# A hybrid attention and delta-rule layer on one core: new operation times in the list that lays out the order of instructions

## The chip, the cores and the metric

One core of a Trainium2 chip. The metric is the device time of one execution in microseconds (us); the median of three runs is given. The engines are TensorE (PE; its weight loads appear as PEld), VectorE (DVE), ScalarE (ACT), GpSimd (POOL) and SyncE (SP), which issues the DMAs. Each runs its own queue of instructions in program order and waits on semaphores for the others.

## The reference

One layer of a streaming encoder over 2048 prompt frames and 32 new frames, D = 1024, in float32. A LayerNorm of the input is projected to 6160 columns. Two branches read them:

```python
qa, ka, va, za, qkv_b, zb, a_b, b_b, gate_a, gate_b = split_projection(x @ w_in)
oa = chunk_band_attention(qa, ka, va, rel_bias)          # 8 heads of 64, band of 9 chunks of 64 frames
ya = (oa * silu(za)) @ w_branch_a
c  = silu(causal_conv(qkv_b, conv_w))                    # width 4; q and k are then L2-normalised
ob = gated_delta_rule(qb, kb, vb, g, beta, state)        # chunks of 64 frames, 8 heads
yb = (rms_norm(ob) * silu(zb)) @ w_branch_b
mix = sigmoid(gate_a) * ya + sigmoid(gate_b) * yb
y = layer_norm(ALPHA * x + mix @ w_out)
```

The delta rule takes a triangular solve for each chunk (all chunks independent), and then a recurrence over chunks:

```python
t_inv = triangular_solve(eye + m, eye)
v_new = u_c - w_c @ s
o_c   = (q_c * exp(gc_c)) @ s + qk_c @ v_new
s     = s * exp(g_last) + k_dec.T @ v_new
```

## The kernel before

**Staging.** The sequence is cut in two halves of 1024 frames (the second also has the 32 new frames). For each half the kernel runs the delta-rule branch (`phase_b`), then attention (`phase_a`). The input projection is cut into 48 column blocks of 128 and one of 16; each block of each half is a "job" whose weights are fetched, split into a high and a low fp16 part (`whi`, `wlo`), and multiplied as three fp16 products (hi·hi, hi·lo, lo·hi) into a PSUM bank `pj` of up to 512 columns. Jobs are the filler of PE: their order is written by hand (`ORDER`, `FILL`, `HEAD`, `TAIL`: 16 delta-rule jobs in the order q, k, v, z, with gate jobs between and behind them, then 16 attention jobs, then the remaining gate jobs). In the second half the branch products run in fp32r beside attention, and the output projection and last LayerNorm close the kernel.

**Delta-rule phase.** For each of 4 head pairs and 2 blocks of 8 chunks: the convolution (three DVE steps on tile `acc`), the decays, products of keys and queries out of PSUM (`p_c`, `qk_bd`, `kd_bd`, `v_t`), a forward substitution on DVE (`substitute`: for 31 columns one product into `sys_t` and one subtraction from `sys_u`, up to some 76 elements a lane; two systems can be in work at once), and the recurrence (`chain`). A step of the recurrence for a chunk is a loop of three hops between PE and DVE: matmul of the state into tile `x`, DVE step `r`; matmul into `x`, DVE step `vn`; matmul into `x`, DVE step `state`. Two more matmuls a chunk go into tile `o`, which ACT copies to `v_t`. There are 128 chunks of the prompt (two heads in each) and 4 of the new frames, so 132. An fp32 matmul appears as two records in the trace.

**What sets the order.** No instruction order is written out. Every activity is a Python generator, a stream, with a clock. `Flow` is a planner: it keeps a heap of streams and always resumes the one with the earliest clock. When a stream issues an instruction, `Flow.spend` (line 194) sets the instruction's planned end: the later of the stream's clock plus a hop and the engine's planned free time, plus a cost from `Engine.price` (line 232). That end becomes the clock of the stream and the free time of the engine. The hops are constants: 0.1 us to PE, 0.2 us to another engine, 0.12 us to the same engine. DMAs have planned landing times too (`Flow.transfer`), and gates hand out buffers and PSUM banks in planned time. The order in which streams are resumed is the program order of every engine's queue and of the DMA queue; nothing else of the plan is in the program. On the chip each instruction waits for its real inputs, behind everything that stands before it in its queue.

**What the change touches.** `Engine.price` alone. It returns microseconds from the operation's name, sizes and memory: on PE from the columns that stream (n) and the result rows (m) by type; on ACT and DVE from a fixed part, larger or smaller when an operand lies in PSUM (`far`), and the elements per lane n at 1200 or 960 (1920) per us; on GpSimd (key `"G"`) likewise. All instructions pass through line 267, in the helper `call`, so that the profile shows L267 for nearly every line; instructions are told apart by tile.

Of the kernel before, what the change touches and what calls it, by code (L numbers as in the profile page):

```python
# [13 lines left out]
F16 = mybir.dt.float16  # L14
# [7 lines left out]
P = 128  # L22
D = 1024
KD = D // P
# [6 lines left out]
HD = 64  # L31
# [187 lines left out]
def width(ap):  # L219
    n = 1  # L220
    for k in ap.shape[1:]:
        n *= k
    return n


class Engine:
# [5 lines left out]
    def price(self, name, a, k):  # L232

        if self.key == "PE":
            n, m = width(a[2]), width(a[1])
            if name == "transpose":
                n = m = max(a[1].shape[0], m)
            if a[1].dtype == F16:
                return max(n / 2400.0, m / 4800.0)
            if a[1].dtype == F32R:  # L240
                return n / 2400.0
            return max(n, m) / (1200.0 if name == "transpose" else 600.0)
        ins = [k[x] for x in ("in_", "in0", "in1") if x in k] or list(a[1:2])
        out = k["out"] if "out" in k else a[0]
        n = width(ins[0] if name in ("bn_stats", "tensor_reduce") else out)
        far = any(getattr(x, "space", None) == PSUM for x in ins + [out])
        if self.key == "G":
            if k.get("op") == ALU.pow:
                return 0.55 + 0.125 * n
            return 0.03 + n / 1200.0 if name == "memset" else 0.1 + n / (960.0 if name == "affine_select" else 480.0)  # L250
        more = sum(not isinstance(k.get(x, 0.0), (int, float, type(None)))
                   for x in ("scale", "bias", "accum_out", "scalar1", "scalar2"))
        if self.key == "S":

            table = k.get("func") == AF.Ln
            if "func" in k and table != self.table and k["func"] != AF.Copy:
                self.table = table
                return 1.28 + self.price(name, a, k)
            return (0.05 if far else 0.093) + 0.093 * more + n / 1200.0
        fast = name in ("tensor_copy", "tensor_scalar") and not far  # L260
        return (0.125 if far else 0.068) + 0.06 * more * fast + n / (1920.0 if fast else 960.0)

    def __getattr__(self, name):
        f = getattr(self.eng, name)
# [2277 lines left out]
```

## Time and profile before

| | |
|---|---|
| Median of 3 runs | 1968.77 us (1964.63 to 1972.47) |
| The profiled execution's own time | 1967.06 us |
| Its span, first to last instruction | 1965.2 us |
| Instructions in it | 40968 |
| DMA | 274.61 MB, 140 GB/s on average |

A profile line of a group names line, engine, operation, result<-inputs and shapes, then the count, busy time in us and mean length of one in ns, and behind the second bar the time its engine sat idle just before, with who released it. Lines of the timeline begin with start and length in us. A matmul's record is longer than its step to the next matmul, since matmuls are pipelined; so the busy time of PE also covers part of the time it waits. In lines on waits stand the total in us, how many times, and in some views the longest.

### The profile page before, as it was taken

To read this page: it belongs to the slowest core of one execution; us is meant where nothing else is said; L and a number is where in the kernel's file an instruction comes from. 1 tells how busy PE (TensorE), PEld (TensorE's weight loads), DVE (VectorE), ACT (ScalarE), POOL (GpSimd) and SP (SyncE) were. 2 spreads that over 40 slices of the span, in tenths; PEclk is the share of its full clock that TensorE was granted. 3 is DMA by queue.
4 is the path that set the end of the run, shared out by engine and by line. 5 is a ranking of instruction groups with operands and counts; after the bars stand their busy time and mean duration, and the time that the engine had idled before them with its cause. 6 is when DMAs were issued, how large, how long until landed. Compare 5 with 4: busy or idle time off the path is not lost. (4 is left out here: it accounts for less than half of the span.)

```text
span 1965.2 us, 40968 instructions
## 1 busy us (share of the span) xinstructions
PE 1894.8 (96%) x14513; PEld 1339.0 (68%) x14513; DVE 1409.0 (72%) x4401; ACT 993.6 (51%) x2022; POOL 771.2 (39%) x1079
## 2 busy tenths in 40 slices
PE   8999999999999998999999999999999999999998
PEld 5445666676455556666776777768877667988886
DVE  7689989973378768679898987355556565465797
ACT  6665545544586777565544444354446575321110
POOL 7344334433344445444344333422222233243673
PEclk9999999999999999999999999999999999999999
DMA  3234232333368887223233233477878798996552
GB/s 134 69 89 114 78 108 68 84 90 105 115 154 203 179 185 168 75 81 84 58 79 93 67 91 103 120 206 189 223 190 172 184 198 187 263 331 200 179 183 89
DMA packets 382950, 274.61 MB, mean 140 GB/s; under 512 B 248339, under 2 KB 319359, under 8 KB 382745
## 3 DMA queue, kind: packets, MB, share of 16 engines
q1 hardware_dynamic: 382744, 272.00, 51.9%
q8 instruction: 114, 1.87, 0.4%
q14 instruction: 92, 0.75, 0.1%
HBM read 157.15 MB, written 71.76 MB: 116 GB/s over the span
## 5 line engine op out<-in xcount | busy, mean ns | idle before, releaser
L267 PE MATMUL pj<-hi,whi 128*128 128x512 f16 (+2 forms) x1992 | 643.0, 338 | 11.6 <-DVE zb L267 3.1
L267 PE MATMUL pj<-hi,wlo 128*128 128x512 f16 (+2 forms) x1952 | 634.5, 338 | 0.6 <-POOL wlo L267 0.5
L267 PEld LDWEIGHTS <-whi 128*128 128x128 f16 x3984 | 408.8, 104 | 229.0 <-issue 9.6
L267 POOL TENSOR_TENSOR wlo<-wraw,whi 128x256 f16<-128x256 f32 (+1 forms) x392 | 281.4, 740 | 466.9 <-ACT whi L267 380.7
L267 PE MATMUL pj<-lo,whi 128*128 128x512 f16 (+2 forms) x1992 | 453.0, 338 | 0.0
L267 PEld LDWEIGHTS <-wlo 128*128 128x128 f16 x1952 | 204.9, 105 | 116.2 <-issue 13.2
L267 ACT ACTIVATE sb<-sb,mx,unit 128x640 f32<-128x640 f32 (+4 forms) x128 | 108.6, 849 | 101.1 <-DVE mx L267 96.0
L267 POOL TENSOR_TENSOR pu<-sb,pu 128x640 f16<-128x640 f32 (+2 forms) x64 | 82.2, 1284 | 177.6 <-ACT pu L267 135.5
L267 ACT ACTIVATE wraw<-wraw,w_scale 128x1024 f32<-128x1024 f32 (+1 forms) x98 | 111.4, 1137 | 78.1 <-DVE w_scale L267 75.8
L267 ACT CAST whi<-wraw 128x512 f16<-128x512 f32 (+2 forms) x212 | 128.2, 611 | 28.0 <-PE pj L267 24.9
L267 DVE TENSOR_TENSOR sys_u<-sys_u,sys_t 128x60 f32<-128x60 f32 (+24 forms) x527 | 124.8, 242 | 5.7
L267 DVE SCALAR_TENSOR_TENSOR acc<-raw,cwT,acc 128x512 f32<-128x512 f32 x144 | 112.4, 781 | 7.9 <-ACT acc L267 6.5
L267 DVE TENSOR_TENSOR sys_t<-sys_u,sys_p 128x60 f32<-128x60 f32 (+21 forms) x459 | 110.6, 244 | 5.5
L267 ACT CAST mh<-sf 128x256 fp32r<-128x256 f32 x64 | 25.7, 406 | 158.3 <-PE c L267 78.1
L267 ACT COPY v_t<-o 128x64 f32<-128x64 f32 x132 | 27.7, 210 | 142.1 <-PE o L267 105.5
L267 DVE CUSTOM_DVE_ANT_0 sb<-a,bias 128x320 f32<-128x320 f32 (+5 forms) x136 | 66.2, 498 | 45.1 <-PE a L267 42.5
L267 POOL TENSOR_TENSOR w_scale<-w_scale,mhalf 128x1 f32<-128x1 f32 x49 | 32.0, 652 | 155.7 <-DVE w_scale L267 118.0
L267 PE MATMUL b<-ghi,whi 128*128 128x256 f32 (+1 forms) x320 | 89.3, 311 | 1.2 <-DVE cr L267 1.1
L267 POOL TENSOR_TENSOR ml<-sf,mh 128x256 fp32r<-128x256 f32 x60 | 59.5, 993 | 77.3 <-PE c L267 51.5
L267 ACT ACTIVATE sig<-pj,w_half 128x512 f32<-128x512 f32 (+2 forms) x84 | 49.3, 587 | 75.7 <-PE pj L267 70.3
L267 ACT CAST pu<-sb 128x640 f16<-128x640 f32 (+4 forms) x128 | 82.2, 650 | 0.7
L267 PEld LDWEIGHTS <-pt 128*128 128x128 f16 x1680 | 65.8, 98 | 23.3 <-issue 6.0
(389 smaller groups left out, 4202.9 us busy)
## 6 DMA issues: line engine op xcount, KB each, us to landing
wraw<-in_w_in SPq DMA_DIRECT2D x192, 256.0 KB
sf<-sig SPq DMA_DIRECT2D x112, 128.0 KB
sig<-sig SPq DMA_DIRECT2D x44, 256.0 KB
sg<-sig SPq DMA_DIRECT2D x37, 256.0 KB
sig<-sg SPq DMA_DIRECT2D x37, 256.0 KB
sys_p<-sol_p SPq DMA_DIRECT2D x68, 128.0 KB
x<-in_x_p SPq DMA_DIRECT2D x16, 512.0 KB
xt<-in_x_p SPq DMA_DIRECT2D x16, 512.0 KB
```

Of the source, the lines that this page charges most:

```text
L267: r = f(*a, **k)
```

## The change

Only numbers in `Engine.price` change. On PE: fp16 matmuls get 2.5 ns more; fp32r matmuls are priced at 2300 columns per us plus 6 ns; fp32 transposes get 2 ns more; other fp32 matmuls no longer go by the larger of n and m, but by n, with a floor, 50 ns more where n is the head size 64, and a branch for 32 or fewer result rows. On ACT: 0.13 us more for operations of 1024 elements a lane, and for fp16 results of 64 lanes out of PSUM. On DVE: 0.16 us more for `bn_aggr`; 0.035 us more for two-tensor operations out of PSUM and for three-dimensional ones with fewer than 32 elements in the last dimension on 128 lanes; for `scalar_tensor_tensor` of 512 elements 0.05 us less out of PSUM and 0.06 us more otherwise. The set of instructions, the tiles and the job order stay.

```diff
             if a[1].dtype == F16:
-                return max(n / 2400.0, m / 4800.0)
+                return max(n / 2400.0, m / 4800.0) + 0.0025
             if a[1].dtype == F32R:
-                return n / 2400.0
-            return max(n, m) / (1200.0 if name == "transpose" else 600.0)
+                return n / 2300.0 + 0.006
+            if name == "transpose":
+                return max(n, m) / 1200.0 + 0.002
+            if m <= 32:
+                return 0.064 + n / 1200.0 * (n > 32)
+            return max(n / 600.0, 0.112) + 0.006 + 0.05 * (n == HD)
...
-            return (0.05 if far else 0.093) + 0.093 * more + n / 1200.0
+            wide = 0.13 if n == KD * P or far and out.dtype == F16 and out.shape[0] == HD else 0.0
+            return (0.05 if far else 0.093) + 0.093 * more + n / 1200.0 + wide
         fast = name in ("tensor_copy", "tensor_scalar") and not far
-        return (0.125 if far else 0.068) + 0.06 * more * fast + n / (1920.0 if fast else 960.0)
+        cost = (0.125 if far else 0.068) + 0.06 * more * fast + n / (1920.0 if fast else 960.0)
+        if name == "bn_aggr":
+            cost += 0.16
+        if name == "tensor_tensor":
+            cost += 0.035 if far or len(out.shape) > 2 and out.shape[-1] < 32 and out.shape[0] == P else 0.0
+        if name == "scalar_tensor_tensor" and n == 512:
+            cost += -0.05 if far else 0.06
+        return cost
```

## The prediction

> **What bounds the kernel now.** I read the totals first, then the clock, then busy time by stage, then who waits for whom inside the stages that lose time.
>
> ```profile
> span 1965.2 us, 40968 instructions
> ...
> PE 1894.8 (96%) x14513; PEld 1339.0 (68%) x14513; DVE 1409.0 (72%) x4401; ACT 993.6 (51%) x2022; POOL 771.2 (39%) x1079
> ```
>
> ```profile
> core 0: 1965.2 us, clock 0.989
> ```
>
> TensorE is the bound: it has nothing in flight for only 1965.2 - 1894.8 = 70.4 us, and a mean clock of 0.989 costs it 1.1% of 1965.2, about 21.6 us. The list of times changes no work, so only such losses can be won. The next view has one row per stage: first delta-rule phase, first attention, second delta-rule phase, second attention with the early branch products, output. After the stretch and its length stand busy times with instruction counts of PE, PEld, DVE, ACT and POOL, then the clock, the DMA share and GB/s.
>
> ```profile
> 100.00:490.00 390.00, 375.18 (x2776) 247.13 (x2774) 317.38 (x1192) 200.03 (x402) 155.69 (x264) 0.99 0.33 91
> 490.00:890.00 400.00, 388.41 (x2901) 229.02 (x2900) 271.19 (x838) 281.27 (x532) 170.88 (x238) 1.00 0.59 143
> 890.00:1260.00 370.00, 355.86 (x3106) 268.58 (x3104) 310.40 (x1175) 167.84 (x383) 135.83 (x238) 0.98 0.32 83
> 1260.00:1720.00 460.00, 450.30 (x4026) 349.34 (x4025) 255.59 (x765) 242.60 (x497) 131.65 (x142) 1.00 0.80 201
> 1720.00:1966.00 246.00, 233.94 (x1184) 195.41 (x1182) 182.32 (x243) 36.81 (x93) 123.44 (x123) 0.98 0.59 195
> ```
>
> In both delta-rule stages DVE is almost full too: 317.38 + 310.40 = 627.8 of 760 us. In them PE has 390 - 375.18 + 370 - 355.86 = 29.0 us with nothing in flight. But a matmul's record overlaps the next one's, so a short stall hardly shows as idle. It shows where the weight load (PEld) waits. The matmuls of the recurrence write tile x; these are the rows of its view on who waited for its results, or for a DVE step between them:
>
> ```profile
> who waited for it (us, times):
>   PEld x L267: 60.0, 161
> ...
>   PE x L267: 10.9, 31
> ```
>
> Next, single instructions (start, length) of PE in one place, the length of 64 output matmuls in the chain that ended last, and two pairs of neighbours on DVE:
>
> ```profile
> 424.87 0.33 PE L267 MATMUL x<-state,k_bd 128*128 128x64 f32 x2
> 425.04 0.38 PE L267 MATMUL pj<-hi,whi 128*128 128x512 f16 x1
> 425.25 0.38 PE L267 MATMUL pj<-hi,wlo 128*128 128x512 f16 x1
> 425.47 0.38 PE L267 MATMUL pj<-hi,whi 128*128 128x512 f16 x1
> ```
>
> ```profile
> 1927.60 14.75 PE a L267 x64
> ```
>
> ```profile
> 332.62 0.74 DVE L267 SCALAR_TENSOR_TENSOR acc<-raw,cwT,acc 128x512 f32<-128x512 f32 x1
> 333.28 0.17 DVE L267 TENSOR_TENSOR sys_u<-sys_u,sys_t 128x16 f32<-128x16 f32 x1
> 333.37 0.20 DVE L267 TENSOR_TENSOR sys_t<-sys_u,sys_p 128x48 f32<-128x48 f32 x1
> 333.49 0.27 DVE L267 TENSOR_SCALAR vn<-x,sc 128x64 f32<-128x64 f32 x1
> ```
>
> A projection matmul takes a record of 0.38 us but a step of 0.215; so 0.165 us of a weight load's wait is covered by the matmul still in flight. The 161 waits of 60.0 / 161 = 0.373 us thus cost about 161 x (0.373 - 0.165) = 33.5 us. Ends: 10.9 us, by PE's row alone, and 60.0 + 10.9 = 70.9 us, if nothing were covered. I take 33.5. It is the largest loss that one group of prices can touch.
>
> **What the change does, part by part.** Every instruction stays; its place in its engine's queue may move, DMA issues with it. PE prices first, old and new list against the rows. A projection matmul of 512 columns goes from 0.2133 to 0.2158, measured 0.215. An fp32r matmul of 512 goes from 0.2133 to 0.2286, measured 14.75 / 64 = 0.2305. A recurrence matmul (64 columns, fp32, both passes) goes from 0.2133 to 0.168, measured 425.04 - 424.87 = 0.17. All three are right now. They alter when the plan believes PE free, but PE is fed to the full by the projections in either order: no gain by themselves.
>
> DVE is where the old list was short. The rows of the page:
>
> ```profile
> L267 DVE TENSOR_TENSOR sys_u<-sys_u,sys_t 128x60 f32<-128x60 f32 (+24 forms) x527 | 124.8, 242 | 5.7
> L267 DVE SCALAR_TENSOR_TENSOR acc<-raw,cwT,acc 128x512 f32<-128x512 f32 x144 | 112.4, 781 | 7.9 <-ACT acc L267 6.5
> L267 DVE TENSOR_TENSOR sys_t<-sys_u,sys_p 128x60 f32<-128x60 f32 (+21 forms) x459 | 110.6, 244 | 5.5
> ```
>
> ```profile
> L267 DVE TENSOR_TENSOR p_c<-b,gcb 128x256 f32<-128x256 f32 x33 | 13.9, 422 | 4.3 <-PE b L267 3.8
> ...
> L267 DVE TENSOR_TENSOR v_t<-b,swap 64x256 f32<-64x256 f32 x32 | 13.5, 422 | 0.7
> ```
>
> Records overlap here too: sys_t began at 333.37, ran 0.20, and the next began 0.12 later, so 0.08 is shared. The substitution's operations occupy 0.242 - 0.08 = 0.162 us on average. The old list gives the form of 60 elements 0.068 + 60/960 = 0.1305, the new 0.1655. For 527 + 459 = 986 of them the plan gains 986 x 0.035 = 34.5 us. The convolution step occupies 333.28 - 332.62 = 0.66; old 0.601, new 0.661: 144 x 0.06 = 8.6 us. Products out of PSUM (from the p_c row to the v_t row, 33 + 66 + 4 x 32 = 227 by the loops) get 0.035 each: 7.9 us. Together 51 us, 8% of the 627.8 us that DVE is busy in the two stages. That is the sense of the change: the old plan let DVE run 8% too fast exactly where it is nearly full. It put the recurrence's matmuls where their DVE step should have been done, and DVE was still behind. With the new list the plan puts more projection matmuls in front of them.
>
> How much goes? Not all: a fixed price removes the mean lateness and not its scatter. Ends: 0 (all scatter) and -33.5 (all mean). I take half, **-17 us**. What is late next is the scatter, below. The plan itself makes the delta-rule phase no longer for PE: projection jobs stand between it and the next attention phase in either order.
>
> Against it, the recurrence's own loop. From a recurrence matmul to the DVE step on it, and from that to the next matmul:
>
> ```profile
> 428.89 0.33 PE L267 MATMUL x<-r,u_bd 128*128 128x64 f32 x2
> ```
>
> ```profile
> 429.26 0.28 DVE L267 TENSOR_SCALAR vn<-x,sc 128x64 f32<-128x64 f32 x1
> ```
>
> ```profile
> 336.00 0.27 DVE L267 SCALAR_TENSOR_TENSOR r<-x,negc,v_t 128x64 f32<-128x64 f32 x1
> ```
>
> ```profile
> 336.33 0.43 PE L267 MATMUL x<-r,u_bd 128*128 128x64 f32 x2
> ```
>
> 0.37 + 0.33 = 0.70 us measured. The old plan has 0.213 + 0.2 (hop) + 0.192 + 0.1 = 0.705, the new 0.660: now 40 ns short. There are 132 chunks x 3 hops = 396. Ends: 0, and 396 x 0.04 = 15.8 us if each hop were placed without slack. A recurrence matmul goes in at the end of some projection matmul, at random within its 0.215 us step, so 40 ns matter in 40/215 of the cases, by 20 ns on average: 396 x 0.186 x 0.02 = 1.5 us. I take **+1**, near the lower end for that reason.
>
> One new price is wrong by the trace:
>
> ```profile
> L267 PE MATMUL a<-part,qs 64*32 64x512 f32 x16 | 8.3, 601 | 0.0
> ```
>
> These are 8 matmuls in two passes, 8.3 / 8 = 1.04 us each with overlap; the old list says 0.853, the new 0.49 (its branch for 32 result rows). The plan thinks PE free up to 0.55 us too early, 8 times: 0 to +4.4 us. They stand in the second attention stage, where PE has filler work, so **+1**.
>
> ACT: wide copies get 0.13 us more.
>
> ```profile
> L267 ACT ACTIVATE wraw<-wraw,w_scale 128x1024 f32<-128x1024 f32 (+1 forms) x98 | 111.4, 1137 | 78.1 <-DVE w_scale L267 75.8
> ```
>
> That is 98 x 0.13 = 12.7 us on an engine busy 281.27 of 400 us where it is fullest: nothing, covered by its idle time; without that cover 12.7 us would come due over the kernel, of either sign for PE.
>
> Last, the clock. Long stalls cost twice:
>
> ```profile
> PE pj L267 <- ACT vf L267: 2.1, 1, 2.1
> ...
> PE pj L267 <- DVE zb L267: 3.1, 1, 3.1
> ```
>
> ```profile
> 612.00:616.00 4.00, 1.62 (x19) 1.08 (x20) 4.00 (x9) 3.81 (x10) 1.75 (x3) 1.00 0.63 190
> 616.60:620.00 3.40, 3.40 (x10) 1.22 (x9) 3.33 (x14) 1.74 (x3) 0.00 (x0) 0.50 0.50 146
> ```
>
> The wait of 2.1 us for vf is followed by 3.4 us at half clock, another 1.7 us. If the new order loses one such wait more than it makes, that is **-1 us**; ends -8 and +8 of the 21.6. The Trainium skill, "TensorE: Matmul & The Clock Gate", section on why this matters for kernels, asks for no idle gaps over about 3 us; a 2.1 us wait was enough here, so the trace and the Trainium skill differ, and by the Trainium skill this term would be 0 and the sum -15.
>
> Sum: -17 + 1 + 1 - 1 = -16 us. The profiled execution took 1967.06 us, 1.7 below the median of 1968.77; on the median the forecast is 1968.8 - 16 = **1953 us** (-0.8%).
>
> **The rivals.** First: the lateness is scatter, and nothing changes. For it:
>
> ```profile
> L267 DVE TENSOR_TENSOR sys_u<-sys_u,sys_t x527: 154/214/728, 132.2 to 1215.0; 128x60 f32<-128x60 f32 x16, 128x54 f32<-128x54 f32 x14, 128x66 f32<-128x66 f32 x13, 128x28 f32<-128x28 f32 x12
> ```
>
> ```profile
> 325.83 0.60 DVE L267 TENSOR_TENSOR sys_u<-sys_u,sys_t 128x42 f32<-128x42 f32 x1
> ```
>
> ```profile
> 325.70 1.30 POOL L267 TENSOR_TENSOR wlo<-wraw,whi 128x256 f16<-128x256 f32 x2 [3.50 <-ACT whi L267]
> ```
>
> The median is 0.214, the mean 0.242, the longest 0.728; an operation of 42 elements took 0.60 us while POOL worked on two tensors. So much of the missing price is a few long blocks, which a fixed price spreads over all 986 and foretells for none. Then -17 becomes about 0: 1968.8 + 1 + 1 - 1 = 1970 us. Against it: even the median, less 0.08, leaves 0.134, and convolution and PSUM products are short in every instance. The Trainium skill, "SBUF — State Buffer", summary of rules for kernel authors, says that a two-input DVE operation and a GpSimd one reading SBUF block each other wholly; the 0.60 us row agrees. That the queues hardly change, because the job order is written by hand, ends here too.
>
> Second, slower: the shorter loop decides. If DVE's queue is not what makes the recurrence late, the 45 ns taken off each recurrence matmul only bring each next one to PE too soon, and all 396 hops pay 40 ns: 1968.8 + 15.8 = 1985 us. It decides once waits before tile x rise above the present 70.9 us. For it: the loop is short by the rows. Against it: the 0.215 us grid, and DVE's longer prices push those same matmuls back.
>
> **How the numbers follow.** Forecast (1953, own range 1928 to 1962): 0.56. Its lower end is all 33.5 us and most of the clock's 8; its upper end a third of the gain. Scatter (1970, 1960 to 1980): 0.25. Loop (1985, 1976 to 2000): 0.19. The range of 8 in 10 leaves out the far half of the loop case and a little below: 1930 to 1983. About 0.5%, or 10 us, is what a measurement of this kernel tells from no change. Faster by more (under 1959): nine tenths of the forecast's 0.56, 0.51. Slower (over 1978.6): 0.18 of the loop's 0.19 and 0.02 of the scatter's, 0.20. Within: the rest, 0.29.
>
> **What would show it.** Right: the weight loads' 60.0 us before tile x fall to 30 to 45, PE's idle in the delta-rule stages from 29.0 to about 20, each projection step stays 0.215, and the attention and output stages keep their length within 4 us. Scatter: the 60.0 stays within 10. Loop: it rises to 75 or more, with r and vn starting 0.37 after their matmul. Wrong altogether: a difference that lies in the attention stages, or a new wait of several us at a passage between phases with a half-clock stretch behind it.

## The result: no change that counts

| | before | after |
|---|---|---|
| Median, 20 runs of each | 1967.78 us (1964.50 to 1973.75) | 1972.26 us (1967.38 to 1983.72) |
| Ratio after / before | | 1.0022, 95% interval 1.0012 to 1.0032 |
| The profiled execution's own time | 1967.06 us | 1971.92 us |

Slower by 0.2%: inside the 0.5% called no change, inside the range 1930 to 1983, and 19 us above the forecast of 1953. One run of before (5015.88 us) and one of the old list by 0.998 (4734.65 us) stand far above all others; the comparisons leave them out, and so do the span given here for before and that list's median below.

The profile of after, read in the order used for before: totals, clock, and the rows by stage (busy time and count of PE, PEld, DVE, ACT, POOL; then clock, DMA share, GB/s). Line L267 has become L279.

```profile
span 1970.1 us, 40943 instructions
...
PE 1887.1 (96%) x14516; PEld 1349.0 (68%) x14516; DVE 1407.6 (71%) x4401; ACT 994.4 (50%) x2022; POOL 773.2 (39%) x1079
```

```profile
core 0: 1970.1 us, clock 0.982
```

```profile
100.00:490.00 390.00, 379.72 (x2803) 254.59 (x2802) 315.23 (x1185) 202.76 (x406) 159.58 (x262) 0.98 0.33 92
490.00:890.00 400.00, 381.54 (x2838) 224.89 (x2837) 270.95 (x833) 274.51 (x522) 167.90 (x238) 0.98 0.59 143
890.00:1260.00 370.00, 362.28 (x3251) 279.92 (x3249) 314.01 (x1188) 177.46 (x400) 143.07 (x247) 1.00 0.32 86
1260.00:1720.00 460.00, 440.30 (x3920) 341.84 (x3919) 254.21 (x763) 238.55 (x490) 126.85 (x138) 0.98 0.79 200
1720.00:1971.00 251.00, 236.03 (x1201) 199.19 (x1199) 180.98 (x246) 37.13 (x94) 123.52 (x124) 0.98 0.58 192
```

PE is busy 7.7 us less in a span 4.9 us longer: nothing is in flight for 83.0 us instead of 70.4. Stage by stage its idle time moved so: in the two delta-rule stages 29.0 to 10.28 + 7.72 = 18.0, in the first attention stage 11.6 to 18.5, in the second 9.7 to 19.7, in the output stage 12.1 to 15.0; what is left of the 12.6, +3.8, came in the first 100 us. The clock costs 1.8% of 1970.1 = 35.5 us instead of 21.6 (some of it falls into idle time, so the two aren't to be added). The waits in the recurrence fell as the prediction hoped, and the other stages lost as much again. The gain, in the view of who waited for tile x:

```profile
who waited for it (us, times):
...
  PEld x L279: 38.1, 121
...
  PE x L279: 6.8, 15
```

60.0 us in 161 waits have become 38.1 in 121. By the prediction's formula that is 121 x (38.1 / 121 - 0.165) = 18.1 us in place of 33.5: 15.4 us won (by the formula; PE's own row fell by 4.1 us only). Yet neither recurrence ended sooner. Tile x's own view says when the first and the last matmul of the third hop ran, in the first half (window 100 to 700 us) and in the second (850 to 1350 us), first in before, then in after:

```profile
L267 PE MATMUL x<-vn,kd_bd x128: 219/275/323, 200.0 to 478.7; 128*128 128x64 f32 x128
...
L267 PE MATMUL x<-vn,kd_bd x136: 219/275/323, 949.5 to 1241.1; 128*128 128x64 f32 x136
```

```profile
L279 PE MATMUL x<-vn,kd_bd x128: 217/275/421, 214.6 to 487.8; 128*128 128x64 f32 x128
...
L279 PE MATMUL x<-vn,kd_bd x136: 219/275/323, 961.0 to 1246.0; 128*128 128x64 f32 x136
```

Both recurrences became shorter, by 278.7 - 273.2 = 5.5 us and by 291.6 - 285.0 = 6.6 us. But they began 14.6 and 11.5 us later, and so ended 9.1 and 4.9 us later. The late start belongs to the prices: the first recurrence's first matmul into x stands at 191.0 to 195.8 us in the five draws of the old list below, and at 201.9 to 210.9 us in the four of the new one. Which price makes it, and how, was not tried.

What PE did with the time it no longer waited is in the busy time of projection matmuls alone (tile pj, PE only) up to 1240 us and in the passage to the second attention phase, 1240 to 1330, of before and then of after:

```profile
890.00:1240.00 350.00, 263.54 (x1296) 0.98 0.31 83
...
1240.00:1330.00 90.00, 61.99 (x382) 0.98 0.64 178
```

```profile
890.00:1240.00 350.00, 281.40 (x1451) 1.00 0.32 88
1240.00:1330.00 90.00, 53.22 (x288) 0.94 0.61 169
```

Between 890 and 1240 us it did 17.9 us more of projections, and it had 8.8 us less of them in the passage. A part of the 17.9 is only made up for, since after had done less of them by 890 us (the same view from the start, before and then after):

```profile
0.00:890.00 890.00, 725.67 (x3143) 0.99 0.45 116
0.00:1240.00 1240.00, 989.20 (x4437) 0.99 0.41 107
```

```profile
0.00:890.00 890.00, 718.50 (x3087) 0.98 0.44 116
0.00:1240.00 1240.00, 999.91 (x4536) 0.98 0.41 108
```

So by 1240 us PE is ahead by 999.91 - 989.20 = 10.7 us of projections. In the passage it then stops. The same two stretches with all engines, before and after:

```profile
890.00:1240.00 350.00, 335.86 (x2958) 254.49 (x2956) 302.52 (x1147) 161.04 (x370) 124.67 (x222) 0.98 0.31 83
1240.00:1330.00 90.00, 85.82 (x613) 61.65 (x611) 41.15 (x108) 43.14 (x86) 31.55 (x41) 0.98 0.64 178
```

```profile
1240.00:1330.00 90.00, 79.95 (x603) 57.50 (x602) 48.13 (x126) 42.79 (x89) 31.61 (x39) 0.94 0.61 169
...
890.00:1240.00 350.00, 342.28 (x3093) 265.23 (x3091) 304.71 (x1154) 170.02 (x385) 131.92 (x231) 1.00 0.32 88
```

PE gains 6.4 us of busy time in the first stretch and loses 5.9 in the second, where the clock falls too. In the view of who waited for whom from 1240 to 1330 us, before and then after, most of the loss is one wait:

```profile
PE pj L267 <- ACT part L267: 1.4, 1, 1.4
```

```profile
PE pj L279 <- ACT part L279: 5.9, 1, 5.9
```

In the timeline of PE in after, the matmuls behind that wait have records of 0.63 us at steps of 0.425 where 0.38 and 0.215 are usual:

```profile
1269.28 1.09 PE L279 MATMUL pj<-lo,whi 128*128 128x272 f16 x8
1276.28 0.58 PE L279 MATMUL pj<-hi,whi 128*128 128x512 f16 x1 [5.91 <-ACT part L279]
1276.66 0.63 PE L279 MATMUL pj<-hi,wlo 128*128 128x512 f16 x1
1277.08 0.63 PE L279 MATMUL pj<-hi,whi 128*128 128x512 f16 x1
```

ACT was late for this reason (its timeline in after):

```profile
1264.72 1.19 ACT L279 ACTIVATE kst<-pj 64x512 f16<-64x512 f32 x2 [3.61 <-PE pj L279]
1268.22 1.32 ACT L279 CAST ghi<-glo 128x256 fp32r<-128x256 f32 x4 [2.31 <-DMA glo<-g]
1269.45 1.13 ACT L279 CAST whi<-wraw 128x512 fp32r<-128x512 f32 x2
1270.49 1.32 ACT L279 CAST ghi<-glo 128x256 fp32r<-128x256 f32 x4
1271.84 1.56 ACT L279 ACTIVATE kst<-pj 64x272 f16<-64x272 f32 x4
...
1275.74 0.49 ACT L279 ACTIVATE part<-pj,w_inv 128x272 f32<-128x272 f32 x1 [1.60 <-DVE part L279]
```

PE's wait ends with ACT's step into `part` at 1275.74, which empties a projection bank. In ACT's queue this step stands behind casts of the delta rule's output (ghi), and these waited 2.31 us for a DMA that brings what the recurrence had only just produced; the step then waited 1.60 us more for one of DVE. PE had come to the attention jobs while the end of the delta-rule phase was still running through the other queues.

### The profile page after: what moved, and what is told of

It is laid out like the page before. It is cut to its first block, busy times and chain, and to the rows that moved or that the text cites. A ratio compares the mean times of both kernels' runs of the same rounds, so it can differ in the third digit from the quotient of the medians.

```text
span 1970.1 us, 40943 instructions
## 1 busy us (share of the span) xinstructions
PE 1887.1 (96%) x14516; PEld 1349.0 (68%) x14516; DVE 1407.6 (71%) x4401; ACT 994.4 (50%) x2022; POOL 773.2 (39%) x1079
## 5 line engine op out<-in xcount | busy, mean ns | idle before, releaser
L279 PE MATMUL pj<-hi,whi 128*128 128x512 f16 (+2 forms) x1992 | 645.2, 339 | 13.3 <-ACT part L279 6.5
L279 PE MATMUL pj<-hi,wlo 128*128 128x512 f16 (+2 forms) x1952 | 636.8, 339 | 0.5 <-POOL wlo L279 0.5
L279 PEld LDWEIGHTS <-whi 128*128 128x128 f16 x3984 | 408.5, 104 | 223.9 <-issue 10.0
L279 PE MATMUL pj<-lo,whi 128*128 128x512 f16 (+2 forms) x1992 | 450.6, 339 | 0.0
L279 POOL TENSOR_TENSOR wlo<-wraw,whi 128x256 f16<-128x256 f32 (+1 forms) x392 | 277.9, 731 | 419.2 <-ACT whi L279 333.5
L279 PEld LDWEIGHTS <-wlo 128*128 128x128 f16 x1952 | 205.5, 105 | 119.1 <-issue 16.0
L279 ACT ACTIVATE sb<-sb,mx,unit 128x640 f32<-128x640 f32 (+4 forms) x128 | 108.7, 850 | 90.8 <-DVE mx L279 84.4
L279 POOL TENSOR_TENSOR pu<-sb,pu 128x640 f16<-128x640 f32 (+2 forms) x64 | 81.5, 1274 | 183.1 <-ACT pu L279 130.1
L279 ACT ACTIVATE wraw<-wraw,w_scale 128x1024 f32<-128x1024 f32 (+1 forms) x98 | 111.4, 1136 | 75.3 <-DVE w_scale L279 70.7
L279 ACT CAST whi<-wraw 128x512 f16<-128x512 f32 (+2 forms) x212 | 128.2, 611 | 40.3 <-PE pj L279 37.3
L279 DVE TENSOR_TENSOR sys_u<-sys_u,sys_t 128x66 f32<-128x66 f32 (+23 forms) x527 | 122.1, 241 | 4.6
L279 DVE SCALAR_TENSOR_TENSOR acc<-raw,cwT,acc 128x512 f32<-128x512 f32 x144 | 111.3, 773 | 7.8 <-ACT acc L279 6.6
L279 ACT CAST mh<-sf 128x256 fp32r<-128x256 f32 x64 | 26.0, 406 | 166.5 <-PE c L279 95.0
L279 DVE TENSOR_TENSOR sys_t<-sys_u,sys_p 128x60 f32<-128x60 f32 (+21 forms) x459 | 106.4, 237 | 4.2
L279 DVE CUSTOM_DVE_ANT_0 sb<-a,bias 128x320 f32<-128x320 f32 (+5 forms) x136 | 66.5, 497 | 54.0 <-PE a L279 48.8
L279 POOL TENSOR_TENSOR w_scale<-w_scale,mhalf 128x1 f32<-128x1 f32 x49 | 33.8, 689 | 172.6 <-DVE w_scale L279 159.1
L279 ACT COPY v_t<-o 128x64 f32<-128x64 f32 x132 | 27.8, 210 | 143.7 <-PE o L279 108.6
L279 PE MATMUL b<-ghi,whi 128*128 128x256 f32 (+1 forms) x336 | 94.3, 312 | 1.3 <-ACT v_s L279 1.3
L279 PEld LDWEIGHTS <-pt 128*128 128x128 f16 x1680 | 66.8, 99 | 30.2 <-issue 7.2
L279 POOL TENSOR_TENSOR ml<-sf,mh 128x256 fp32r<-128x256 f32 x60 | 58.6, 979 | 70.0 <-PE c L279 38.9
L279 ACT ACTIVATE sig<-pj,w_half 128x512 f32<-128x512 f32 (+2 forms) x84 | 49.2, 586 | 71.5 <-PE pj L279 64.2
L279 PE MATMUL b<-ghi,wlo 128*128 128x256 f32 (+1 forms) x336 | 84.7, 284 | 0.0
```

The source lines that it names most:

```text
L279: r = f(*a, **k)
```

## The experiments

Two theories. **Drained filler:** the new prices keep PE from waiting in the recurrence by putting more projections in front of its matmuls; the delta-rule phase ends no earlier than before, so these projections are only taken from what PE needs at the passage. Then the lower waits go with every layout under the new prices, so does the loss at the passage, and one more filler job there wins it back. **Chance:** any change of the prices lays out 40,000 instructions anew, and which waits meet is luck; then the old prices scaled by a thousandth would do as much. A third is the prediction's rival, the loop that is 40 ns short. Scaling multiplies what `call` hands to `spend` and leaves the hops alone. The figures of the draws stand together behind the last run; "passage" is PE's busy time from 1240 to 1330 us.

**Parts of the change.** The PE prices alone, with ACT and DVE as before (shown against after, cut at the dots):

```diff
-            return (0.05 if far else 0.093) + 0.093 * more + n / 1200.0 + wide
+            return (0.05 if far else 0.093) + 0.093 * more + n / 1200.0
...
-        return cost
+        return (0.125 if far else 0.068) + 0.06 * more * fast + n / (1920.0 if fast else 960.0)
```

> Only the PE prices of the change. Theory 1 (the DVE prices free the recurrence; PE then comes too early to the passages between phases): without them the weight loads before tile x wait as before, 55 to 65 us (60.0 before, 38.1 after), and the time is 1965 to 1980 us. Theory 2 (any new list reshuffles the queues, and the sum moves by chance): the waits before x may move by over 10 us either way, and the time by up to 15 us either way.

1986.86 us, ratio 1.0101 (1.0078 to 1.0123). Waits before x 53.4: the PE prices, said to bring nothing by themselves, took 6.6 us of waits and yet made the slowest part. The ACT and DVE prices alone (against after):

```diff
-                return n / 2300.0 + 0.006
-            if name == "transpose":
-                return max(n, m) / 1200.0 + 0.002
-            if m <= 32:
-                return 0.064 + n / 1200.0 * (n > 32)
-            return max(n / 600.0, 0.112) + 0.006 + 0.05 * (n == HD)
+                return n / 2400.0
+            return max(n, m) / (1200.0 if name == "transpose" else 600.0)
```

> Only the DVE and ACT prices of the change. Theory 1: the waits of weight loads before tile x fall to 35 to 45 us as in the changed kernel, and long PE waits at the passages come up as there, so 1960 to 1973 us. Theory 2: no bond between the waits before x and the DVE prices; waits of 45 to 65 us, time up to 15 us either way.

1971.94 us, 1.0019 (1.0006 to 1.0031), waits 45.4, passage 81.05 with a wait of 4.9 us for `part`: two thirds of the lower waits and most of the loss at the passage come with these prices. Only the 0.035 us of the substitution, on the old list:

```diff
-        return (0.125 if far else 0.068) + 0.06 * more * fast + n / (1920.0 if fast else 960.0)
+        cost = (0.125 if far else 0.068) + 0.06 * more * fast + n / (1920.0 if fast else 960.0)
+        if name == "tensor_tensor" and not far:
+            cost += 0.035 if len(out.shape) > 2 and out.shape[-1] < 32 and out.shape[0] == P else 0.0
+        return cost
```

> Only one price of the change: 0.035 us more for the substitution's two-tensor operations. It is two thirds of what the change adds to DVE in the delta-rule phases. Theory 1: the waits before tile x fall by about two thirds of what the whole change took from them, to 42 to 50 us; time 1955 to 1970 us. Theory 2: as for the others, waits of 45 to 65 us without pattern.

1966.28 us, 0.9991 (0.9979 to 1.0002), waits 53.4, passage 84.53. The prediction took two thirds of the missing 51 us (34.5) from here, so waits of 42 to 50 were due; it was 6.6 of the whole fall of 21.9, in one draw.

**The layout as such.** The old list, every price scaled:

```diff
-            self.flow.spend(self.key, self.price(name, a, k))
+            self.flow.spend(self.key, 1.002 * self.price(name, a, k))
```

> The list of before with every price multiplied by 1.002: no price becomes better or worse by more than a few ns. Theory 1: waits before tile x stay at 55 to 65 us, time within 5 us of before. Theory 2: the order is reshuffled all the same, and the time moves by 5 to 15 us either way, as much as the change itself moved any stage.

1988.03 us, 1.0095 (1.0079 to 1.0110). The same line with 0.998:

> The list of before with every price multiplied by 0.998. Theory L (the old list's order is a lucky draw among many, and the true cost of its wrong DVE prices is hidden by that luck): 1975 to 1995 us like the factor 1.002, waits of weight loads before tile x at 55 to 65 us. Rival T (1.002 hit one bad spot, and the old list is ordinary): 1960 to 1972 us.

1976.77 us, 1.0045 (1.0028 to 1.0061). With 1.001:

> The list of before with every price multiplied by 1.001. Theory L: 1972 to 1995 us, waits before tile x at 55 to 65 us. Rival T: 1960 to 1972 us.

1975.71 us, 1.0051 (1.0033 to 1.0069). With 0.999:

> The list of before with every price multiplied by 0.999, one more draw. If the unchanged list is a lucky draw: waits before tile x 55 to 65 us, time 1972 to 1990 us. If it is ordinary: under 1972 us.

1974.92 us, 1.0029 (1.0018 to 1.0040). No price became truer or falser by a thousandth, and the time moved by 7 to 20 us, always up. The waits before x stayed at 61.9 to 64.8. Now the new list, with 1.002, 0.998 and 0.999:

> The changed list with every price multiplied by 1.002. Theory L: the corrected DVE prices keep the waits before tile x low in any draw, 33 to 48 us, and the time is 1960 to 1980 us, around the changed kernel's own 1972. Rival T: waits before x go back to 50 to 65 us in a new draw, time as for the old list's draws.

1985.22 us, 1.0083 (1.0066 to 1.0101).

> The changed list with every price multiplied by 0.998. Theory L: waits before tile x 33 to 48 us, time 1960 to 1980 us. Rival T: waits of 50 to 65 us, time as for the old list's draws.

1968.27 us, 0.9999 (0.9988 to 1.0009).

> The changed list with every price multiplied by 0.999, one more draw. If the mean over draws is what the change moves: waits before tile x 33 to 48 us, a wait of 4 us or more near the passage at 1270 us, time 1965 to 1985 us.

1966.83 us, 0.9996 (0.9979 to 1.0014). Waits 39.4 to 40.8 in all three, passage 78.1 to 80.2 of 90 us, PE's wait for `part` 5.6 to 6.9 us. Time is a matter of the draw, these three are not.

**The passage.** In the second half one more gate job goes ahead of the attention jobs, from behind them, with the new list:

```diff
-HEAD, TAIL = [2, 3], [6, 5]
+HEAD, TAIL = [2, 3], [6, 6]
```

> The changed list, and one more gate job as filler between the second delta-rule phase and the second attention phase (the second entry of TAIL 5 to 6; the same jobs, one moved). Theory P (with the new DVE prices PE works projections off earlier and meets the attention jobs while the delta-rule phase still runs; that is the loss at this passage): the 5.9 us wait of PE for the part tile near 1270 us goes, PE's waits between 1200 and 1300 us fall by 6 to 10 us, waits before tile x stay 33 to 48 us, time 1958 to 1970. Rival D (that wait is one more accident of a draw): another wait of the same size takes its place, time 1966 to 1985.

1963.42 us, 0.9976 (0.9963 to 0.9989). The waits stay at 38.8; the passage in its row:

```profile
1240.00:1330.00 90.00, 84.64 (x619) 60.29 (x618) 45.09 (x126) 42.24 (x88) 31.77 (x41) 0.98 0.59 164
```

4.7 us of busy time are back, and the clock with them. The 5.9 us wait for `part` is gone. A wait of 4.4 us for a DVE step of the attention (mx), which after doesn't have here, stands some 36 us further on, so this draw alone doesn't rule out rival D. On ACT the delta rule's output has now arrived when its casts come up (timeline of this kernel):

```profile
1277.42 0.48 ACT L279 ACTIVATE vf<-pj,w_inv 128x272 f32<-128x272 f32 x1
1277.81 2.53 ACT L279 CAST ghi<-glo 128x256 fp32r<-128x256 f32 x8
1280.24 0.62 ACT L279 CAST whi<-wraw 128x512 f16<-128x512 f32 x1
1282.02 1.19 ACT L279 ACTIVATE kst<-pj 64x512 f16<-64x512 f32 x2 [1.16 <-PE pj L279]
```

The 2.31 us for the DMA are gone, and the first kst copy waits for PE. The same edit on the old list:

> The old list with the one gate job more between the second delta-rule phase and the second attention phase: the control for that edit. Theory P (the passage loses only under the new DVE prices): PE's waits from 1240 to 1330 us stay at 8 to 10 us, nothing to win, time 1966 to 1985 by the draw. Rival G (the extra filler is good by itself, whatever the list): time 1958 to 1964.

1976.32 us, 1.0052 (1.0029 to 1.0074); passage 86.02 against 85.82: nothing to win there with the old prices. Two more draws of the new list with the extra job, prices by 0.999 and 1.001:

> The changed list, the gate job moved, every price times 0.999: a second draw of that kernel. Theory P: waits from 1240 to 1330 us 8 to 12 us instead of the 17 to 21 of the changed list's four draws, waits before tile x 33 to 48 us, time 1958 to 1972. Rival D (the first one was an accident): waits at the passage of 15 us or more again.

1964.29 us, 0.9984 (0.9969 to 0.9998); waits 40.5, passage 81.37. The wait for `part` is 2.1 us, but PE has another of 3.5 us for DVE, and little of the passage is won back.

> The same with every price times 1.001: a third draw. Theory P: waits from 1240 to 1330 us 8 to 12 us, waits before tile x 33 to 48 us, time 1958 to 1975. Rival D: waits at the passage of 15 us or more.

1958.21 us, 0.9953 (0.9937 to 0.9969); waits 41.9, passage 87.07. With the waits of weight loads counted in, PE's waits from 1240 to 1330 us are 15.2 to 19.9 us in the four draws without the job (not quite the 17 to 21 expected) and 8.9, 16.7 and 6.3 in the three with it, so the middle one misses its 8 to 12. And one more job ahead of the attention of the first half too, as it stands and with prices by 1.001:

```diff
-HEAD, TAIL = [2, 3], [6, 5]
+HEAD, TAIL = [2, 3], [7, 6]
```

> The changed list with one gate job more at both passages (TAIL 7 and 6). The changed list's first attention phase lost 6 us more than the old list's. If that is the same matter (PE too early at the first passage): PE's waits from 490 to 890 us fall from about 30 to 21 to 24 us and the time is 1955 to 1963. If it is something else (the next half's LayerNorm getting between the scores): they stay at 26 to 32 us, time 1960 to 1975.

1957.69 us, 0.9945 (0.9924 to 0.9966), the fastest of all. PE's waits from 490 to 890 us, weight loads counted in, fell from after's 28.6 to 22.3 us, as the first of the two asked.

> The changed list with one gate job more at both passages, every price times 1.001: a second draw of the fastest kernel so far. If the fillers and the corrected prices together hold in another order: 1955 to 1966 us. If 1957.7 was a lucky draw: 1966 to 1980 us.

1973.20 us, 1.0031 (1.0017 to 1.0045), and 26.9 us of those waits: the lead of the seventh job is not told apart from a lucky draw.

**Single prices and the loop.** Without the 0.13 us for wide ACT operations:

```diff
-            wide = 0.13 if n == KD * P or far and out.dtype == F16 and out.shape[0] == HD else 0.0
+            wide = 0.0
```

> The changed list without the 0.13 us that ACT's wide operations got. Theory P: the passage at 1270 us is DVE's matter, so its wait of over 4 us stays; waits before tile x stay 33 to 48 us; time 1962 to 1985, by the draw. Rival A (the ACT price makes the loss): waits of the weight-scale matmuls in the first 100 us and the one at 1270 us fall by half, time 1955 to 1968.

1976.46 us, 1.0038 (1.0023 to 1.0053), passage 79.51, wait for `part` 6.5: this price isn't what empties the passage. It has a part in the loss at the start: in the first 100 us PE's busy time is 90.08 us, where after has 87.26 and before 91.14, and the waits of its b matmuls for ACT's whi fell from 3.9 to 1.2 us. And the planned hop to PE made longer by 30 of the missing 40 ns:

```diff
-HOP_PE, HOP, HOP_SAME = 0.1, 0.2, 0.12
+HOP_PE, HOP, HOP_SAME = 0.13, 0.2, 0.12
```

> The changed list with the planned hop to PE at 0.13 instead of 0.10 us, so that the recurrence's planned loop is 0.69 instead of 0.66 us, against 0.70 measured. My term (a loop 40 ns short costs about 1.5 us): the 38.1 us that weight loads wait before tile x stay at 33 to 42. The rival of the prediction (the short loop costs up to 15.8 us): they fall to under 30. Time 1965 to 1985 by the draw.

1978.30 us, 1.0045 (1.0027 to 1.0063), waits 37.0 against 38.1. The short loop costs nothing that shows in them.

**All draws together.** Waits of the weight load before x in us; busy time of PE in 890 to 1240 (projections alone in brackets where looked at) and in the passage; PE's wait for `part` there, 0 where there is none. The windows are fixed, and the kernels drift against one another by up to some 25 us at the end of the recurrence, so a single passage figure is rough; the bands are what counts.

| Prices and TAIL | median us | waits | PE 890:1240 | PE 1240:1330 | wait for `part` |
|---|---|---|---|---|---|
| old | 1967.78 | 60.0 | 335.86 (263.5) | 85.82 | 1.4 |
| old, by 0.998, 0.999, 1.001, 1.002 | 1976.77, 1974.92, 1975.71, 1988.03 | 61.9 to 64.8 | 333.95 to 336.52 (261.7 to 269.3) | 84.69 to 86.40 | 0 to 0.3 |
| old, 6 and 6 | 1976.32 | 61.1 | 334.78 (263.6) | 86.02 | 0 |
| new | 1972.26 | 38.1 | 342.28 (281.4) | 79.95 | 5.9 |
| new, by 0.998, 0.999, 1.002 | 1968.27, 1966.83, 1985.22 | 39.4 to 40.8 | 339.18 to 341.48 (277.8 to 279.3) | 78.11 to 80.23 | 5.6 to 6.9 |
| new without 0.13 on ACT; new with the hop | 1976.46; 1978.30 | 41.2, 37.0 | 340.91, 340.23 | 79.51, 81.00 | 6.5, 4.9 |
| new, 6 and 6; by 0.999, 1.001 | 1963.42; 1964.29, 1958.21 | 38.8 to 41.9 | 340.47 to 342.25 | 81.37 to 87.07 | 0 to 2.1 |
| new, 7 and 6; by 1.001 | 1957.69; 1973.20 | 42.5, 35.8 | 338.52, 336.48 | 85.38, 85.69 | 0, 1.4 |

Each band rests on rows like these, of the old list by 1.002 and the new by 1.002: who waited before x, then the passage with all engines, and for the new one the wait for `part`, which the other doesn't have.

```profile
  PEld x L267: 62.0, 166
```

```profile
1240.00:1330.00 90.00, 84.69 (x649) 61.49 (x649) 43.29 (x114) 42.25 (x94) 33.33 (x44) 1.00 0.52 149
```

```profile
  PEld x L279: 39.4, 118
```

```profile
1240.00:1330.00 90.00, 78.11 (x574) 56.24 (x572) 46.56 (x126) 40.28 (x91) 28.81 (x37) 0.94 0.52 150
```

```profile
PE pj L279 <- ACT part L279: 6.7, 1, 6.7
```

The bands of the waits and of the passage at TAIL 6 and 5 do not touch. The wait for `part` parts them most cleanly: 4.9 us or more in all six kernels of the new list with TAIL 6 and 5, and 2.1 or less with the old prices or with the extra job. The projections that PE has done by 1240 us are apart too, 984.7 to 989.2 us in the old list's five draws and 994.4 to 1004.8 in the new list's four. So both the fall of the waits and the loss at this passage belong to the prices: drained filler holds there. Around it lies a scatter of about 20 us that belongs to nothing but the layout. Over their draws the old list has a mean of 1976.6 (five), the new 1973.2 (four), the new with 6 and 6 1962.0 (three). New less old is -3.5 with a standard error of 5.3 (from spreads of 7.3 and 8.4): not told apart. The extra job on the new list is -11.2 with one of 4.6, and on the list as it stands -8.8 us by medians whose intervals are clear of each other; on the old list, in the one draw that was run, it is +8.5 against the unscaled list and 0.3 under the mean of the five. The new list with the extra job lies 14.7 us under the old list's mean, with a standard error of 3.8; that is near the -16 of the forecast, but it takes an edit that the forecast did not have. That the unscaled old list, from which the forecast was made, is the fastest of its five draws, 8.9 us under their mean, is seen and not explained.

## Why the prediction was wrong

- **DVE's prices and the waits in the recurrence (-17): right.** Waits before x forecast at 30 to 45, found 38.1, and by the formula -15.4 us. PE's idle time in the delta-rule stages was to be about 20 and is 18.0. Its rival, that the lateness is only scatter, falls: all new-list draws lie at 35.8 to 42.5. Which prices do it was partly wrong: PE's have a share (6.6), the substitution's is smaller than thought (6.6), and 14.6 come with ACT and DVE together, out of 21.9, by one draw each.
- **What is late next: the step that failed.** It was put so: "The plan itself makes the delta-rule phase no longer for PE: projection jobs stand between it and the next attention phase in either order." A wait removed was booked as time won. But the recurrences, 5.5 and 6.6 us shorter, began later and ended 9.1 and 4.9 us later, and PE put projections into the time: by 1240 us it had done 10.7 us more of them. (That DVE being full is what ends the phase is not shown: in before it was busy 250.23 of the 294.40 us from 946.7 to 1241.1.) These jobs were the ones that stood between the phase and the next attention. With them spent, PE reached jobs whose banks could not be emptied, and 5.9 of the 6.4 us of busy time went back within 90 us, the clock's part on top. One more job there won 8.8 us by the medians, 11.2 by the means, of the 19 us by which the forecast missed; as far as is known, what is left lies in the stages below and in the lucky draw that the forecast started from. The prediction's own list of what would make it wrong altogether has this place: a wait of several us at a passage between phases, half clock behind it. It was not made a rival and got no chance.
- **"The attention and output stages keep their length within 4 us": wrong.** The first attention stage lost 6.9 us of PE's time, the second with the passage 10.0. In the first it is a group of small waits (view of waits on PE, 600 to 640 us, and the stretch itself, both of after):

```profile
PE a L279 <- DVE mx L279: 2.8, 1, 2.8
PE c L279 <- DMA pt<-pu: 2.1, 2, 1.8
PE c L279 <- DVE ob L279: 1.7, 1, 1.7
```

```profile
612.00:628.00 16.00, 8.19 (x68) 4.60 (x68) 15.54 (x51) 10.30 (x19) 8.68 (x11) 0.68 0.86 224
```

  DVE is busy 15.54 of these 16 us and PE 8.19, at a clock of 0.68. How much of that is the prices' is open: PE's busy time in this stage is 386.0 to 389.7 of 400 us in the six draws with the old prices, and 376.2 to 388.8 in the eleven of the new list, so bands that overlap. In the loss of the first 100 us the wide ACT price has a part; the loss in the output stage was not tried.
- **The clock (-1, ends -8 and +8): outside its ends,** 13.9 us worse by the means. It was tied to the count of long waits, which was guessed to fall by one; in the view of PE's waits the groups whose longest is 2 us or more went from 4 to 10. Its reading that a 2.1 us wait was enough for half clock leaves out another wait just ahead (last section). The draws scatter from 0.979 to 0.990, so not all of it is the prices'.
- **All other waits as fixed: wrong, and the range with it.** A new list lays out everything anew, and draws that differ by 0.1% in every price spread over 20 us. The prediction gave "nothing changes" only through scatter in DVE's lateness; it came out of a gain and a loss of like size. That 1972 lies inside 1930 to 1983 is luck: this part of the range was there for scatter and the loop, and neither is what happened.
- **The loop (+1, rival 1985 us): nothing speaks against the small term.** Waits fell instead of rising, and a hop 30 ns longer changed them by 1.1 us. **ACT (0)** and **the wrong price of the 32 rows (+1)** are within what the draws can't tell; the latter was not tried by itself.

## What to carry to other kernels

A wait taken out of a phase is time won only where the phase ends sooner: ask what the freed engine will do instead, and whether that work is missed at the next boundary; if so, the hand-written supply of filler has to be set again with the new plan (here one job more, 0.9976 where the prices alone gave 1.0022). When a planner lays out the order, scale its prices by a thousandth up and down before judging an edit: here that alone moved the time by up to 1%, more than the edit, and single medians with tight intervals compare two draws, not two lists. Sort the effects by a figure that holds over the draws, such as the waits before one tile, and leave the rest as scatter.

## What was not expected of the hardware

In after the clock of PE falls while it still waits and stays low once it runs again. These are the stretches of the 5.9 us gap in after and of the time right behind it; PE's busy time is the second group of numbers, the clock the third from the end:

```profile
1270.40:1276.20 5.80, 0.00 (x0) 0.00 (x0) 4.98 (x10) 4.11 (x12) 4.09 (x4) 0.72 0.70 245
1276.40:1279.80 3.40, 3.40 (x9) 1.18 (x8) 2.12 (x4) 2.09 (x5) 0.00 (x0) 0.50 0.45 90
```

A mean of 0.72 over the gap means half clock for some 3.2 of its 5.8 us, and then 3.4 us at 0.50 in full work, which cost 1.7 us more. In before, the wait for vf that the prediction shows was followed by the same 3.4 us at 0.50, so in both cases the clock cost 1.7 us behind the gap. But the 2.1 us there did not stand alone. The waits of PE from 612 to 616 us, in before:

```profile
PE pj L267 <- ACT vf L267: 2.1, 1, 2.1
PE b L267 <- DVE mx L267: 0.8, 1, 0.8
```

The wait of 0.8 us came less than 1 us before the other, PE was busy 1.62 of these 4 us, and half clock began at about 616.6, when PE had been at work again for 1.3 us. So no single wait of 3 us was needed there; how much idle time is enough, and within what stretch, these two cases don't show.
